# Attention's output projection: from row products over whole blocks to seven block products

## The chip, the cores and the metric

One core of one Trainium2 chip runs the whole program in one launch. TensorE (PE) multiplies, VectorE (DVE) and ScalarE (ACT) work on tiles in SBUF and PSUM, GpSimd (POOL) and SyncE (SP) mostly issue transfers. Each engine runs its own list of instructions, and semaphores join the lists. The metric is device time of one execution in microseconds, the median of several runs.

## The reference, cut to what matters

A decoder trunk of two layers on one sequence of 512 rows and 1024 columns, in fp32. Layer 0 mixes with gated linear attention, layer 1 with strictly causal stick-breaking attention of 16 heads of 64; each is followed by a squared-ReLU MLP (1024 to 4096 to 1024) and LayerNorms. The change is in layer 1:

```python
z = jnp.einsum('bqhd,bkhd->bhqk', q_blk, k_blk) * scale
log_1m = jnp.where(mask, jax.nn.log_sigmoid(-z), 0.0)
rev = lax.cumsum(log_1m, axis=3, reverse=True)
log_w = jax.nn.log_sigmoid(z) + (rev - log_1m)
w = jnp.where(mask, jnp.exp(log_w), 0.0)
outs.append(jnp.einsum('bhqk,bkhd->bqhd', w, v_blk))
...
mix = o.reshape(B, S, D).astype(h.dtype) @ sb_w_o[j]
h = layer_norm(DEEPNORM_ALPHA * h + mix, ln_g[layer, 0], ln_b[layer, 0])
```

The product that is changed is the last but one line: o (512 x 1024) times sb_w_o (1024 x 1024). Its result is added to the residual rows h, which are then normed, transposed and multiplied by the MLP's first weights.

## The kernel before, in words

Every large product is made of three matmuls for each pair of 128-deep operands: a number is split into a high part (ACT's copy to a shorter format, `hi`) and a low part (DVE's subtraction, `lo`), and high times high, high times low and low times high are summed in a PSUM bank. `put` does this for a result in PSUM, `split_tile` for a weight tile of 128 x 1024. There are eight PSUM banks, handed out in turn by `bank()`. `unit()` gives a tile of 4 x 512 columns (they show as T in the profile), `chain()` one of 512 (c).

The 16 heads are taken as eight pairs, 0 to 7. For each pair there are: `keys` and `queries` (products by 128 columns of weights), `scores` (PE, six banks), `weights` (DVE masks the diagonal blocks in PSUM, ACT takes two sigmoids, DVE scans them into the attention weights c), `turn` (PE transposes c into a bank, ACT copies it to `wt`) and `outputs` (PE multiplies the values by wt; the result is the transposed attention output of 128 columns for 512 rows). The loop over p issues, in this order: pair p's turn, woven into PE work that does not depend on it; the weights of pair p+1; the outputs of pair p. `outputs` ended in a `put`. For p up to 5 the turn is woven into the queries of pair p+2. For pairs 6 and 7 there are no more queries, and the first half of the output projection fills their turns: for each tile of 128 rows t, `rows(oA, t, ...)` multiplies the four finished pairs 0 to 3 (oA) by a 512 x 512 block of sb_w_o, 12 matmuls of 128x512, 48 in each turn. After pair 7, `part2(t)` does the second half, pairs 4 to 7, with 24 matmuls for each tile t, and `finish` norms that tile's rows (statistics and centring on DVE, a reciprocal root on POOL) while PE goes on with the next; `turn_affine` then transposes the normed rows (L231), applies gain and bias in ACT's copy (L234) and splits them by `put`, for the MLP's first product `up(0)`. The order from `by_tiles` was: tile 0, tile 1, transposes of 0, tile 2, transposes of 1, tile 3, transposes of 2; tile 3's transposes were done within up(0).

The order on each engine follows the code, save that the splits of a weight tile are set further ahead than their line in it, between the copies and scans that stand there.

## Time and profile before

| | |
|---|---|
| median of 3 runs | 1115.32 us (1114.44 to 1115.41) |
| the profiled execution | 1115.04 us |
| its span, first to last instruction | 1113.3 us |
| granted TensorE clock, mean | 0.999 |
| PE busy | 1105.4 us (99%), 5515 matmuls and transposes |
| DVE busy | 805.8 us (72%) |
| ACT busy | 559.4 us (50%) |
| POOL busy | 131.5 us (12%) |

Matmul rows are pipelined: each reads about 0.39 us, and the start of the next comes earlier than its end, so durations of PE are taken from starts. Times below count from the span's start. In the profile of before, matmul lines are L93 to L95 (the three passes), L934 (scores), L968 (transposes of weights), L982 (outputs), L231 (transposes of normed rows); ACT's are L70 (hi of a weight), L98 (hi of `put`), L955 and L956 (sigmoids), L973 (wt) and L234; DVE's are L72 (lo of a weight), L99 (lo of `put`), L951 (masks), L959 (scans), L167 and L169 (adds to h).

### The profile page before, as it was taken

The page shows a single profiled execution, that of the slowest core. Times are in us where ns is not written, and L with a number is a line of the kernel's source. Part 1 is how long each engine was busy: PE and PEld are TensorE (multiplying, and loading weights), DVE is VectorE, ACT ScalarE, POOL GpSimd, SP SyncE. Part 2 cuts the span into 40 slices and gives each one's busy share as a digit, 9 for nine tenths or more (in the row PEclk, how much of TensorE's full clock was granted, in tenths as well). Part 3 has the DMA queues.
Part 4 walks back from the last instruction along what each step waited for, and adds up shares of the span by engine and source line. Part 5 has one row for each costly group of instructions (what it writes and reads, how often), then busy time and mean ns, then how long its engine had stood idle before and what let it go on. Part 6 is the DMA issues. An engine that isn't in the chain of part 4 may idle for free.

```text
span 1113.3 us, 14363 instructions
## 1 busy us (share of the span) xinstructions
PE 1105.4 (99%) x5515; PEld 916.0 (82%) x5515; DVE 805.8 (72%) x1017; ACT 559.4 (50%) x839; POOL 131.5 (12%) x167
## 2 busy tenths in 40 slices
PE   9999999999999999999999999999999999999997
PEld 7888888898888888888888777778988888888885
DVE  4677639957966856858899786767389767667677
ACT  4455437653533534536675566655445435336363
POOL 1011222200000100122302010001200000001222
PEclk9999999999999999999999999999999999999999
DMA  7441399492670770787845422111946806706773
GB/s 239 132 133 57 114 253 215 123 298 96 188 208 19 199 209 26 195 204 132 245 98 158 116 85 95 58 55 51 291 120 202 234 33 176 221 19 190 183 124 89
DMA packets 108632, 163.81 MB, mean 147 GB/s; under 512 B 13018, under 2 KB 37978, under 8 KB 108564
## 3 DMA queue, kind: packets, MB, share of 16 engines
q1 hardware_dynamic: 85684, 118.34, 32.4%
q0 software_dynamic: 20416, 39.85, 20.4%
q10 hardware_dynamic: 2464, 4.72, 1.1%
q8 instruction: 43, 0.70, 0.2%
q14 instruction: 25, 0.20, 0.1%
HBM read 157.64 MB, written 3.15 MB: 144 GB/s over the span
## 4 chain that ended last, share of the span: by engine, by line
PE 91%; DMA 5%; DVE 1%; issue 1%; POOL 1%; SPq 0%; ACT 0%; POOLq 0%; DVEq 0%
PE ps L355 28%; PE ps L93 18%; PE ps L94 18%; PE ps L95 18%; DMA B<-in_gla_w_o_dram 4%; PE ps L796 3%; PE ps L982 2%; PE ps L968 2%; PE ps L934 2%; PE ps L231 1%; DMA h<-in_x_dram 0%; PE ps L584 0%; POOL B L314 0%; PE ps L121 0%; DVE lo L72 0%
## 5 line engine op out<-in xcount | busy, mean ns | idle before, releaser
L355 PE MATMUL ps<-hi,T 128*128 128x512 f32 x1008 | 313.2, 390 | 0.1
L93 PE MATMUL ps<-T,hi 128*128 128x512 f32 (+1 forms) x776 | 290.1, 374 | 0.0
L94 PE MATMUL ps<-T,hi 128*128 128x512 f32 (+1 forms) x776 | 287.1, 370 | 0.1
L95 PE MATMUL ps<-T,lo 128*128 128x512 f32 (+1 forms) x776 | 286.9, 370 | 0.0
L72 DVE TENSOR_TENSOR lo<-raw,hi 128x1024 fp32r<-128x1024 f32 x130 | 158.0, 1221 | 115.0 <-ACT hi L70 114.7
L355 PEld LDWEIGHTS ps<-hi,T 128*128 128x128 f32 x1008 | 188.9, 188 | 40.0 <-DVE T L99 0.6
L70 ACT ACTIVATE hi<-raw 128x1024 fp32r<-128x1024 f32 x130 | 137.6, 1063 | 166.8 <-PE ps L94 59.2
L70 ACT ACTIVATE hi<-B 128x1024 fp32r<-128x1024 f32 x118 | 124.4, 1059 | 171.2 <-PE ps L94 104.2
L72 DVE TENSOR_TENSOR lo<-B,hi 128x1024 fp32r<-128x1024 f32 x118 | 142.9, 1222 | 84.7 <-ACT hi L70 84.5
L355 PE MATMUL ps<-lo,T 128*128 128x512 f32 x504 | 196.1, 389 | 0.0
L95 PEld LDWEIGHTS ps<-T,lo 128*128 128x128 f32 x776 | 146.2, 188 | 24.8
L93 PEld LDWEIGHTS ps<-T,hi 128*128 128x128 f32 x776 | 146.2, 188 | 24.4 <-issue 0.9
L94 PEld LDWEIGHTS ps<-T,hi 128*128 128x128 f32 x776 | 146.4, 189 | 23.7 <-DVE T L99 0.4
L314 POOL DMA_DIRECT2D B<-in_mlp_w_down_dram x52 | 63.0, 1259 | 544.7 <-DMA B<-in_mlp_w_down_dram 343.6
L355 PEld LDWEIGHTS ps<-lo,T 128*128 128x128 f32 x504 | 94.6, 188 | 19.6
L169 DVE TENSOR_TENSOR h<-h,ps 128x512 f32<-128x512 f32 x110 | 74.9, 682 | 6.9 <-PE ps L95 4.0
L93 PE MATMUL ps<-hi,T 128*128 128x512 f32 x192 | 77.4, 403 | 0.0
L95 PE MATMUL ps<-hi,T 128*128 128x512 f32 x192 | 75.3, 392 | 0.0
L94 PE MATMUL ps<-lo,T 128*128 128x512 f32 x192 | 75.1, 391 | 0.0
L99 DVE TENSOR_TENSOR T<-s,T 128x1024 fp32r<-128x1024 f32 (+1 forms) x50 | 53.4, 1069 | 9.3 <-ACT T L98 9.3
L98 ACT ACTIVATE T<-s 128x1024 fp32r<-128x1024 f32 (+1 forms) x50 | 47.0, 946 | 21.2 <-DVE s L721 14.1
L959 DVE TENSOR_TENSOR_SCAN c<-r,c 128x384 f32<-128x384 f32 (+2 forms) x64 | 48.4, 807 | 3.8 <-ACT c L956 3.8
(190 smaller groups left out, 1195.4 us busy)
## 6 DMA issues: line engine op xcount, KB each, us to landing
raw<-in_mlp_w_up_dram SPq DMA_DIRECT2D x64, 512.0 KB, 5.6
B<-in_mlp_w_down_dram SPq DMA_DIRECT2D x64, 512.0 KB, 5.5
B<-in_mlp_w_down_dram POOLq DMA_DIRECT2D x52, 512.0 KB, 8.0
raw<-in_gla_w_in_dram SPq DMA_DIRECT2D x20, 512.0 KB, 3.9
raw<-in_mlp_w_down_dram SPq DMA_DIRECT2D x16, 512.0 KB, 4.6
B<-in_gla_w_o_dram POOLq DMA_DIRECT2D x14, 512.0 KB, 8.2
raw<-in_kv_w_dram SPq DMA_DIRECT2D x12, 512.0 KB, 4.7
B<-in_gla_w_o_dram SPq DMA_DIRECT2D x8, 512.0 KB, 6.1
```

The costliest lines, as they stand in the source:

```text
L70: keep(nc.scalar.activation(hi, raw, AF.Copy))
L72: keep(nc.vector.tensor_tensor(lo, raw, hi.bitcast(F32), op=ALU.subtract))
L93: keep(nc.tensor.matmul(ps, lhsT=a[0], rhs=b[0], start=first, stop=False))
L94: keep(nc.tensor.matmul(ps, lhsT=a[0], rhs=b[1], start=False, stop=False))
L95: keep(nc.tensor.matmul(ps, lhsT=a[1], rhs=b[0], start=False, stop=last))
L98: keep(nc.scalar.activation(hi, ps, AF.Copy))
L99: keep(nc.vector.tensor_tensor(lo, ps, hi.bitcast(F32), op=ALU.subtract))
L169: nc.vector.tensor_tensor(h, h, ps, op=op)
L314: nc.gpsimd.dma_start(out=b.rearrange("p (a b) -> p a b", a=2), in_=weights(k, h, j), accum_op=ALU.add)
L355: nc.tensor.matmul(banks[s], lhsT=a(k, s)[x], rhs=b[k][y], start=opens and (k, x, y) == (0, 0, 0), stop=closes and (k, x, y) == (3, 1, 0), ...
L796: nc.tensor.matmul(banks[s], lhsT=a(k, s)[x], rhs=b[k][w], start=opens and (k, x, w) == (0, 0, 0), stop=closes and (k, x, w) == (3, 1, 0), ...
L959: nc.vector.tensor_tensor_scan(down, r[:, at][:, ::-1], down, 0.0, op0=ALU.mult, op1=ALU.add)
```

## The change

The 512 x 1024 by 1024 x 1024 product is taken as 2 x 2 blocks: a11, a21 are rows 0 to 255 and 256 to 511 of pairs 0 to 3; a12, a22 the same of pairs 4 to 7; sb_w_o is cut into four 512 x 512 blocks. Seven products of sums of blocks, each of 2 row tiles x 4 depths x 3 passes = 24 matmuls, replace eight of 24.

- Product 1 (a11 by the first block) runs in pair 6's turn, and its two banks are added into or taken off all four row tiles, both halves (eight adds). Transposes of the turn are issued at its steps 3, 4, 6 and 7 (`FILL`). Product 7 (a11 - a21 by a sum of blocks) runs in pair 7's turn.
- The other five, 120 matmuls, run in `project()`, in the order second, sixth, fifth, third, fourth. The row tiles are complete after the fifth (tiles 2 and 3, one half), the third (half of tiles 0, 1) and the fourth. The order handed to `finish` is now: rows 0, 1, 2, transposes of 0, rows 3, transposes of 1; the transposes of 2 and 3 are done within up(0).
- The outputs of pairs 0 to 3 are copied by ACT to o1, unsplit. Those of pairs 4 to 7 are split by `put` as before, and copied once more by ACT to o2. Sums of blocks are taken by DVE from o1 and o2 (`minus`, and a subtraction) and split into five operands (`first`, `seventh`, `sixth`, `fifth`, `third`).
- The sums of weight blocks are built by transfers: `fetch` brings a block to a buffer by a plain transfer on SP, and the following blocks are added by accumulating transfers on POOL. One buffer b22 (two tiles of 128 x 1024, d) takes three, one after another, with its splits between; the buffers of the last k and q take one.
- k and q tiles hold high and low part in one; `differences` uses the d tiles, and there are five c buffers instead of nine.

```diff
+        def outputs(self, steps):
 
             ops = bank()
             for s, (j, i, e) in enumerate(steps):
@@ -983,15 +988,61 @@
                                      lhsT=vs[hd // 8][:, j, DH * (hd % 8):DH * (hd % 8) + DH],
                                      rhs=self.wt[a][:, 512 * j + P * (i - j):512 * j + P * (e - j)], start=(s == 0),
                                      stop=(s == len(steps) - 1), skip_group_check=True)
-            put(hi, lo, ops)
+            return ops
 
     NP = SBH // 2
     TAKE = {4: 2, 5: 1, 6: 1, 7: 1}
 
+    FILL = {3: 1, 4: 1, 6: 1, 7: 1}
+
     LAST = [(0, 2, 4), (1, 2, 4), (2, 2, 4), (3, 3, 4), (0, 0, 1), (0, 1, 2), (1, 1, 2)]
+    LO, HI = slice(0, 256), slice(256, 512)
+    STEPS = [(s, k) for s in range(2) for k in range(4)]
+    LATER = [(s, k) for s in range(2) for k in range(3)] + [(0, 3), (1, 3)]
+    w_o = lambda k, h, j: block(sb_w_o[0], 512 * k + 256 * h, 512 * j)
+
+    def fetch(bs, k, j, onto=False):
+        for h, b in enumerate(bs):
+            to = b.rearrange("p (a b) -> p a b", a=2)
+            if onto:
+                nc.gpsimd.dma_start(out=to, in_=w_o(k, h, j), accum_op=ALU.add)
+            else:
+                nc.sync.dma_start(out=to, in_=w_o(k, h, j))
+
+    def pieces(bs):
+        got = []
+        for b in bs:
+            hi, lo = split_tile(b, 2)
+            got += [(hi[:, i, :], lo[:, i, :]) for i in range(2)]
+        return got
+
+    def into(u, a, ks):
+
+        put(u[:, ks, LO], u[:, ks, HI], a[:, ks, :])
+
+    def halves(u):
+        return lambda k, s: (u[:, k, P * s:P * s + P], u[:, k, 256 + P * s:256 + P * s + P])
+
+    def run(steps, a, b, banks, opens=True, closes=True, mid=None):
+
+        for n, (s, k) in enumerate(steps):
+            if mid:
+                mid(n)
+            if opens and k == 0:
+                banks[s] = bank()
+            for x, y in ((0, 0), (0, 1), (1, 0)):
+                nc.tensor.matmul(banks[s], lhsT=a(k, s)[x], rhs=b[k][y], start=opens and (k, x, y) == (0, 0, 0),
+                                 stop=closes and (k, x, y) == (3, 1, 0), skip_group_check=True)
+
+    def add(s, banks, i, j, first=False, last=False):
+        hs[2 * i + s].add(j, banks[s], first, last, ALU.subtract if j else ALU.add)
+
+    tt = nc.vector.tensor_tensor
+    minus = lambda out, a, b: nc.vector.scalar_tensor_tensor(out, a, -1.0, b, op0=ALU.mult, op1=ALU.subtract)
+
     pairs = [Pair(p) for p in range(NP)]
-    oA = Split(1)
-    parts = [(oA.hi[0][:, i, :], oA.lo[0][:, i, :]) for i in range(4)]
+    o1 = unit(F32)
+    a11, a21 = o1[:, :, LO], o1[:, :, HI]
     vec, vcols = lnvec(0, 1), lncols(1, 0)
     pairs[0].keys(held[0])
     pairs[0].queries(ps=held[1])
@@ -1007,37 +1058,97 @@
             made = pairs[p].turn()
             pairs[p + 2].queries(lambda k: [next(made, None) for _ in range(TAKE.get(k, 0))])
         else:
-            n = p - (NP - 2)
-            pcs = pieces_512(sb_w_o[0], 0, 4, 512 * n)
             made = pairs[p].turn()
-            for t in range(NT):
-                hs[t].add(n, rows(oA, t, pcs, range(4)), True)
-                for _ in range(((0, 1, 2, 2), (1, 1, 2, 1))[n][t]):
-                    next(made, None)
+            fill = lambda n: [next(made, None) for _ in range(FILL.get(n, 0))]
+            ps = [None, None]
+            if p == NP - 2:
+                run(STEPS, halves(first), pieces_512(sb_w_o[0], 0, 4, 0), ps, mid=fill)
+                for s in range(2):
+                    for i in range(2):
+                        for j in range(2):
+                            add(s, ps, i, j, True)
+            else:
+                run(STEPS, halves(seventh), b7, ps, mid=fill)
+                for s in range(2):
+                    for j in range(2):
+                        add(s, ps, 1, j)
+            for _ in made:
+                pass
         if p + 1 < NP:
             pairs[p + 1].weights()
         if p == 1:
             differences(1)
         if p in (1, 2):
             hs[1 + p].affine(vec, tc.keep_in_program_order)
-        if p in (4, 6):
-            u = unit(F32R)
-            parts += [(u[:, i, :], u[:, 2 + i, :]) for i in range(2)]
-        pairs[p].outputs(*parts[p], LAST if p == NP - 1 else [(j, j, NT) for j in range(NT)])
-    pcs = [pieces_512(sb_w_o[0], 512, 4, 512 * n) for n in range(2)]
+        ops = pairs[p].outputs(LAST if p == NP - 1 else [(j, j, NT) for j in range(NT)])
+        if p < 4:
+            nc.scalar.activation(o1[:, p, :], ops, AF.Copy)
+        else:
+            if p == 4:
+                o2, o2h, o2l = unit(F32), unit(F32R), unit(F32R)
+                a12, a22 = o2[:, :, LO], o2[:, :, HI]
+            put(o2h[:, p - 4, :], o2l[:, p - 4, :], ops)
+            nc.scalar.activation(o2[:, p - 4, :], ops, AF.Copy)
+        if p == 3:
+            first = unit(F32R)
+            into(first, a11, slice(0, 4))
+            b22 = wide()
+            fetch(b22, 1, 1)
+            fetch(b22, 0, 1, True)
+        if p == NP - 3:
+            seventh = unit(F32R)
+            for h in range(2):
+                ks, less = slice(2 * h, 2 * h + 2), chain().rearrange("p (a b) -> p a b", a=2)
+                tt(less, a11[:, ks, :], a21[:, ks, :], op=ALU.subtract)
+                put(seventh[:, ks, LO], seventh[:, ks, HI], less)
+            b5 = [both(tag).bitcast(F32).rearrange("p a b -> p (a b)") for tag in ("k", "q")]
+            fetch(b5, 0, 0)
+            fetch(b5, 0, 1, True)
+        if p == NP - 2:
+            b7 = pieces(b22)
+            fetch(b22, 0, 0, True)
+            sixth, fifth = unit(F32R), unit(F32R)
+        if p >= NP - 2:
+            ks = slice(0, 3) if p == NP - 2 else slice(3, 4)
+            tt(a22[:, ks, :], a22[:, ks, :], a21[:, ks, :], op=ALU.subtract)
+            minus(a11[:, ks, :], a22[:, ks, :], a11[:, ks, :])
+            into(sixth, a11, ks)
+            into(fifth, a22, ks)
     h3T = Split()
+    whole = lambda c0: lambda k, s: tuple(o[:, k, c0 + P * s:c0 + P * s + P] for o in (o2h, o2l))
+
+    def project():
+
+        xs, zs, ws = ([None, None] for _ in range(3))
+        run(LATER, whole(0), pieces_512(sb_w_o[0], 512, 4, 0), xs)
+        for s in range(2):
+            add(s, xs, 0, 0, last=True)
+        b6 = pieces(b22)
+        fetch(b22, 1, 0, True)
+        minus(a12, a12, a11)
+        run(STEPS, halves(sixth), b6, zs, closes=False)
+        for s in range(2):
+            add(s, zs, 1, 0)
+        run(STEPS, halves(fifth), pieces(b5), zs, False, False)
+        for s in range(2):
+            add(s, zs, 1, 1, last=True)
+        third = unit(F32R)
+        into(third, a12, slice(0, 4))
+        b3 = pieces_512(sb_w_o[0], 512, 4, 512)
+        b4 = pieces(b22)
+        for s in range(2):
+            run(STEPS[4 * s:4 * s + 4], halves(third), b3, zs, False)
+            add(s, zs, 0, 1, last=True)
+            yield s
+        for s in range(2):
+            run(STEPS[4 * s:4 * s + 4], whole(256), b4, ws)
+            add(s, ws, 1, 0, last=True)
+            yield 2 + s
+            yield ~s
 
     vec = lnvec(1, 0)
 
-    def part2(t):
-        c = slice(P * t, P * t + P)
-        pss = [bank(), bank()]
-        for n, k in ((0, 0), (0, 1), (0, 2), (1, 0), (0, 3), (1, 1), (1, 2), (1, 3)):
-            mm3(pss[n], tuple(o[:, c] for o in parts[4 + k]), pcs[n][k], k == 0, k == 3)
-        for n in range(2):
-            hs[t].add(n, pss[n], False, True)
-
-    late = finish(by_tiles(part2), vcols, hs, h3T, chain)
+    late = finish(project(), vcols, hs, h3T, chain)
     sbx.__exit__(None, None, None)
 
     def done1(steps, work, *_):
```

Three places show what moves. The first is DVE between pair 6's scans (L959 before, L964 now) and the masks of pair 7's scores (L951, L956). Before (T_6117 is the low part of pair 5's outputs, the h rows are the adds of the four row tiles):

```order
L99 TENSOR_TENSOR T_6117<-ps_6300,T_6117 128x512
L167 SCALAR_TENSOR_TENSOR h_1637<-h_1637,ps_6323 128x512
L167 SCALAR_TENSOR_TENSOR h_1638<-h_1638,ps_6337 128x512
L167 SCALAR_TENSOR_TENSOR h_1639<-h_1639,ps_6359 128x512
L72 TENSOR_TENSOR lo_6628<-raw_6624,hi_6626 128x1024
L167 SCALAR_TENSOR_TENSOR h_1640<-h_1640,ps_6386 128x512
L72 TENSOR_TENSOR lo_6634<-raw_6630,hi_6632 128x1024
L951 TENSOR_TENSOR ps_6414<-ps_6414,low 128x128
L951 TENSOR_TENSOR ps_6415<-ps_6415,low 128x128
```

Now, where T_6114 is that low part, c_6300 and c_6304 are the two halves of a11 - a21, T_6299 is the seventh operand and d_5928 is b22:

```order
L99 TENSOR_TENSOR T_6114<-ps_6287,T_6113 128x512
L1102 TENSOR_TENSOR c_6300<-T_5008 128x512
L167 SCALAR_TENSOR_TENSOR h_1637<-h_1637,ps_6326 128x512
L1102 TENSOR_TENSOR c_6304<-T_5008 128x512
L99 TENSOR_TENSOR T_6299<-c_6300,T_6299 128x2x256
L167 SCALAR_TENSOR_TENSOR h_1637<-h_1637,ps_6326 128x512
L99 TENSOR_TENSOR T_6299<-c_6304,T_6299 128x2x256
L167 SCALAR_TENSOR_TENSOR h_1639<-h_1639,ps_6326 128x512 x2
L167 SCALAR_TENSOR_TENSOR h_1638<-h_1638,ps_6353 128x512 x2
L167 SCALAR_TENSOR_TENSOR h_1640<-h_1640,ps_6353 128x512 x2
L956 TENSOR_TENSOR ps_6395<-ps_6395,low 128x128
L956 TENSOR_TENSOR ps_6396<-ps_6396,low 128x128
```

Between T and the masks stood four adds and two weight splits; now twelve operations of 512 columns stand there, and the two weight splits come behind the masks, one ahead of the first scan and one ahead of the last.

The second place is ACT in pair 7's turn, from the copy of pair 6's outputs to the last wt copies. Before:

```order
L98 ACTIVATE T_6480<-ps_6481 128x512 [waits PE_49]
L973 ACTIVATE wt_6518<-ps_6520 128x4x128 [waits PE_49]
L973 ACTIVATE wt_6519<-ps_6540 128x4x128 [waits PE_49]
L973 ACTIVATE wt_6518<-ps_6560 128x3x128 [waits PE_49]
L973 ACTIVATE wt_6518<-ps_6560 128x128
L973 ACTIVATE wt_6519<-ps_6567 128x3x128 [waits PE_49]
L973 ACTIVATE wt_6519<-ps_6567 128x128
L70 ACTIVATE hi_6874<-raw_6872 128x1024 [waits DMAHW2_49,PE_49]
```

Now (T_6112 is o2, hi_6671 the high part of the weight sum in the k tile, T_6483 and T_6484 the sixth and the fifth operand; L978 are the wt copies):

```order
L978 ACTIVATE wt_6502<-ps_6512 128x4x128 [waits PE_49]
L1091 ACTIVATE T_6112<-ps_6461 128x512 [waits DVE_49]
L70 ACTIVATE hi_6671<-k_6308 128x1024 [waits DMASW6_49,PE_49]
L978 ACTIVATE wt_6501<-ps_6525 128x3x128 [waits PE_49]
L978 ACTIVATE wt_6501<-ps_6525 128x128
L978 ACTIVATE wt_6502<-ps_6535 128x3x128 [waits PE_49]
L98 ACTIVATE T_6483<-T_5008 128x3x256 [waits DVE_49]
L98 ACTIVATE T_6484<-T_6112 128x3x256 [waits Activation_49]
L978 ACTIVATE wt_6502<-ps_6535 128x128
L978 ACTIVATE wt_6501<-ps_6549 128x2x128 [waits PE_49]
L978 ACTIVATE wt_6502<-ps_6549 128x2x128
```

A copy to o2 that waits for DVE, a weight split and two high parts came among the wt copies; the two splits of weights of before, of which the first row is shown, follow the wt copies. In pair 6's turn the o2 copy and the two halves of T_6299 stand among the wt copies in the same way.

The third place is PE at the end of the projection. Before, the last part2 matmuls, the transposes of tile 2 and up(0)'s first:

```order
L93 MATMUL ps_6807<-hi_6632,T_6480 128x512
L94 MATMUL ps_6807<-lo_6634,T_6480 128x512
L95 MATMUL ps_6807<-hi_6632,T_6480 128x512
L231 MATMUL ps_6845<-ident,h_1639 128x128 x4
L231 MATMUL ps_6857<-ident,h_1639 128x128 x4
L93 MATMUL ps_6896<-T_6636,hi_6874 128x256
L94 MATMUL ps_6896<-T_6637,hi_6874 128x256
L95 MATMUL ps_6896<-T_6636,lo_6876 128x256
```

Now the fourth product's last matmuls, the transposes of tile 1 (h_1638) and up(0) with the first transposes of tile 2 (h_1639):

```order
L1034 MATMUL ps_6820<-hi_6728,T_6113 128x512
L1034 MATMUL ps_6820<-lo_6730,T_6113 128x512
L1034 MATMUL ps_6820<-hi_6728,T_6114 128x512
L231 MATMUL ps_6843<-ident,h_1638 128x128 x4
L231 MATMUL ps_6855<-ident,h_1638 128x128 x4
L93 MATMUL ps_6894<-T_6580,hi_6872 128x256
L93 MATMUL ps_6895<-T_6580,hi_6872 128x256
L93 MATMUL ps_6896<-T_6580,hi_6872 128x256
L93 MATMUL ps_6897<-T_6580,hi_6872 128x256
L231 MATMUL ps_6947<-ident,h_1639 128x128 x3
L94 MATMUL ps_6894<-T_6581,hi_6872 128x256
L95 MATMUL ps_6894<-T_6580,lo_6874 128x256
```

Tile 1's transposes, which had a row tile's 24 matmuls behind them, now stand directly ahead of up(0), and those of tile 2 are in up(0).

More of the change, by code (lines that the diff above doesn't have):

```diff
@@ L887, in chain, with wide @@
     def chain():
-        return sbp.tile([P, S], F32, tag="c", bufs=9, name=nm("c"))
+        return sbp.tile([P, S], F32, tag="c", bufs=5, name=nm("c"))
+    def wide():
+        return [sbp.tile([P, 2 * S], F32, tag="d", bufs=2, name=nm("d")) for _ in range(2)]
     def differences(n):
-        v, shifted = vs[n], [chain() for _ in range(NT)]
+        v, shifted = vs[n], [d[:, at] for d in wide() for at in (slice(0, S), slice(S, 2 * S))]
         nc.gpsimd.memset(shifted[0][0:1, :], 0.0)
@@ L903, in yoco_kernel, with both @@
     HALVES = ((A0, A1), (A1, A0))
+    def both(tag):
+        return sbp.tile([P, 2, S], F32R, tag=tag, bufs=2, name=nm(tag))
     class Pair:
@@ L909, in __init__ @@
             self.p = p
-        def part(self, tag):
-            return sbp.tile([P, S], F32R, tag=tag, bufs=2, name=nm(tag))
         def keys(self, ps=None):
             ps = ps or cols(h2T, piece_128(kv_w, P * self.p))
-            self.k = self.part("kh"), self.part("kl")
+            k = both("k")
+            self.k = k[:, 0, :], k[:, 1, :]
             put(*self.k, ps)
@@ L920, in queries @@
             ps = ps or cols(h2T, piece_128(sb_w_q[0], P * self.p), mid)
-            self.q = qh, ql = self.part("qh"), self.part("ql")
+            q = both("q")
+            self.q = qh, ql = q[:, 0, :], q[:, 1, :]
             nc.scalar.activation(qh, ps, AF.Copy, scale=DH ** -0.5)
@@ L974, in turn @@
                 yield
-        def outputs(self, hi, lo, steps):
+        def outputs(self, steps):
             ops = bank()
```

## Prediction

> **What bounds the kernel now.** I read the page's totals first, then the stretches around the change, then each engine's order of time in them.
>
> ```profile
> PE 1105.4 (99%) x5515; PEld 916.0 (82%) x5515; DVE 805.8 (72%) x1017; ACT 559.4 (50%) x839; POOL 131.5 (12%) x167
> PE 91%; DMA 5%; DVE 1%; issue 1%; POOL 1%; SPq 0%; ACT 0%; POOLq 0%; DVEq 0%
> ...
> 712.40:730.20 17.80, 17.80 (x109) 13.98 (x108) 12.60 (x21) 10.69 (x22) 0.00 (x0) 1.00 0.09 31
> 730.20:748.10 17.90, 17.90 (x111) 13.96 (x110) 12.32 (x22) 10.96 (x26) 0.00 (x0) 1.00 0.19 60
> 748.10:775.00 26.90, 26.90 (x150) 22.28 (x149) 18.72 (x29) 12.47 (x27) 2.38 (x6) 1.00 0.13 40
> ```
>
> PE is 91% of the chain that ended last. The three stretches are pair 6's part, pair 7's part and the rest of the projection (length, then busy time of PE, PEld, DVE, ACT, POOL, granted clock): PE never stops in them, while DVE works 12.6 of 17.8 us and ACT 10.7. So a matmul removed is time gained, and a wait that PE meets is time lost one for one: later stages have no idle PE time to absorb it. The DMA share of 0.09 to 0.19 leaves transfers out of the bound.
>
> The PE rows give the price of a matmul and the points that PE reaches:
>
> ```profile
> 719.01 0.39 PE L93 MATMUL ps<-hi,T 128*128 128x512 f32 x1
> 721.73 0.39 PE L93 MATMUL ps<-hi,T 128*128 128x512 f32 x1
> 730.22 0.50 PE L934 MATMUL ps<-kh,qh 64*128 64x512 f32 x2
> 732.33 2.37 PE L982 MATMUL ps<-wt,T 128*64 128x512 f32 x16
> 747.56 0.60 PE L968 MATMUL ps<-ident,c 128*128 128x128 f32 x4
> 748.08 2.39 PE L982 MATMUL ps<-wt,T 128*64 128x256 f32 x28
> 750.40 0.50 PE L93 MATMUL ps<-hi,T 128*128 128x512 f32 x1
> 774.14 1.03 PE L231 MATMUL ps<-ident,h 128*128 128x128 f32 x8
> 774.93 0.36 PE L93 MATMUL ps<-T,hi 128*128 128x256 f32 x1
> ```
>
> Twelve matmuls lie between the first two starts: 2.72 / 12 = 0.227 us each, though a row reads 0.39. The rest are pair 7's scores, pair 6's outputs, pair 7's last transposes, its outputs, the start of the rest of the projection, the last transposes ahead of up(0), and up(0)'s first matmul.
>
> **The gain.** Seven products of 24 replace 192 matmuls by 168: 24 x 0.227 = -5.5 us. But each of the last two turns goes from 48 to 24, so PE asks for the next thing 24 x 0.227 = 5.5 us earlier in pair 6's turn and 10.9 us earlier at the end of pair 7's, and gives 5.5 us back afterwards. Without any wait PE would reach pair 7's scores at 724.8, its last transposes at 736.7, its outputs at 737.2, the remaining products at 739.5. What must be ready there is made by DVE and ACT:
>
> ```profile
> 719.34 3.59 DVE L959 TENSOR_TENSOR_SCAN c<-r,c 128x384 f32<-128x384 f32 x6
> 722.85 0.67 DVE L99 TENSOR_TENSOR T<-ps,T 128x512 fp32r<-128x512 f32 x1
> 723.43 1.27 DVE L167 SCALAR_TENSOR_TENSOR h<-h,ps 128x512 f32<-128x512 f32 x2
> ...
> 730.92 1.22 DVE L72 TENSOR_TENSOR lo<-raw,hi 128x1024 fp32r<-128x1024 f32 x1
> 732.06 0.49 DVE L951 TENSOR_TENSOR ps<-ps,low 128x128 f32<-128x128 f32 x2
> 733.56 1.23 DVE L959 TENSOR_TENSOR_SCAN c<-r,c 128x512 f32<-128x512 f32 x1 [1.01 <-ACT c L956]
> ...
> 738.03 2.42 DVE L959 TENSOR_TENSOR_SCAN c<-r,c 128x384 f32<-128x384 f32 x4
> 740.38 0.66 DVE L99 TENSOR_TENSOR T<-ps,T 128x512 fp32r<-128x512 f32 x1
> ```
>
> In before, pair 7's masks (732.06) begin 1.8 us after its scores and its last scan ends at 740.4, 7 us before PE transposes it at 747.56. That slack is what the change spends.
>
> **The waits.** I walk the new order with these durations.
>
> *DVE ahead of pair 7's masks.* From the low part T at 722.85 to the masks there now stand thirteen 128x512 operations (T, two a-differences and their low parts, eight h adds), each 0.60 (722.85 to 723.43, and 1.27 for two): 13 x 0.60 = 7.8, so masks at 730.7, 5.9 us after PE wants to write those scores. From masks to the last scan's end before took 740.4 - 732.1 = 8.3, of which 1.0 was waiting on ACT; two weight splits (1.2 each, 1.14 apart) now lie between the scans: 8.3 - 1.0 + 2.3 = 9.6, less some overlap with ACT. The last scan ends at about 740.2, the same instant as before, while PE's need for it has moved to 736.7 plus the waits so far.
>
> ```profile
> 720.48 0.73 ACT L98 ACTIVATE T<-ps 128x512 fp32r<-128x512 f32 x1
> 723.05 0.60 ACT L973 ACTIVATE wt<-ps 128x512 f32<-128x512 f32 x1 [1.85 <-PE ps L968]
> ...
> 728.09 1.06 ACT L70 ACTIVATE hi<-raw 128x1024 fp32r<-128x1024 f32 x1 [0.66 <-PE ps L95]
> 729.45 1.06 ACT L70 ACTIVATE hi<-raw 128x1024 fp32r<-128x1024 f32 x1 [0.30 <-PE ps L95]
> 730.42 1.19 ACT L973 ACTIVATE wt<-ps 128x384 f32<-128x384 f32 x4
> ```
>
> *ACT in pair 6's turn.* The new copy of the outputs to o2 waits for DVE's T (done 723.5), and what stands behind it waits too: copy 0.5, half of the seventh operand's high part 0.5, a wt copy 0.5, the other half (its a-difference, DVE's fourth operation, ends at 725.3) to 725.9, a weight split 0.96, then the wt copies that free the next score bank, at 727.5. PE stands in pair 7's scores at 725.4: **2.1 us**. Two more wt copies (0.55), a split (0.96) and the last wt pair (0.5) end at 729.5; PE is ready for outputs at 728.8: **0.8 us**.
>
> *Pair 7's turn.* PE then comes to the last transposes at 736.7 + 2.9 = 739.4 or so; the scan ends 740.2: **0.9 us**. At pair 7's outputs (740.5) ACT has just got past its next o2 copy, which waited for DVE's T behind the last scan (740.8): copy 0.5, split 0.96, three wt columns 0.4 give 742.9: **2.4 us**, and **0.2** for the next. Inside these outputs the high parts of the sixth and fifth operands stand ahead of three wt copies. They wait for two h adds and two 768-wide DVE subtractions after T (2 x 0.6 + 2 x 0.9 past 740.8: 743.9), take 0.7 each, and the copies come at 745.7: **1.1 us** in three pieces. Outputs end at about 746.5 rather than 739.5.
>
> *The five products after.* They run without a wait. An accumulating transfer and its neighbours land in:
>
> ```profile
> B<-in_gla_w_o_dram POOLq DMA_DIRECT2D x14, 512.0 KB, 8.2
> raw<-in_sb_w_o_dram SPq DMA_DIRECT2D x8, 512.0 KB, 3.5
> ```
>
> The second sum in the shared buffer is issued as soon as pair 7's product weights have been split out of it, ahead of pair 6's scores at 712, and is read at 725.9; the third is issued after DVE's two splits (732.3 and 739.7) and read at 756.4 and 757.8, 8 us beyond the 8.2 it takes; the sum in the k and q tiles is issued near 719 and read at 741. They cost nothing on this path. On POOL's queue the last of them stands at 740, ahead of the LayerNorm work of the first tile near 768; on SP's the two plain fetches of the k/q sum stand between weights of up(0) that are read near 762 and later. Early in the attention the shifted copies of the second half wait sooner, which may hold one w_q fetch: 0 to 0.7 us at pair 3's keys; I take 0.
>
> *LayerNorm into up(0).* Before, 24 matmuls stood between the transposes of tile 1 and of tile 2, and only tile 3 went into up(0). Now tile 1's transposes stand directly ahead of up(0), whose first matmul reads them:
>
> ```profile
> 775.09 1.89 ACT L234 ACTIVATE c<-ps,bcol,gcol 128x128 f32<-128x128 f32 x5
> 776.80 0.69 ACT L98 ACTIVATE T<-c 128x512 fp32r<-128x512 f32 x1
> 778.45 1.08 POOL L183 TENSOR_SCALAR ve<-mv 128x1 f32<-128x1 f32 x1 [7.82 <-DVE mv L182]
> 779.62 0.57 POOL L184 TENSOR_TENSOR rs<-ve,mhalf 128x1 f32<-128x1 f32 x1
> 780.22 0.81 DVE L190 TENSOR_SCALAR h<-h,mv,rs 128x1024 f32<-128x1024 f32 x1 [0.77 <-POOL rs L184]
> ```
>
> From the first affine row to the end of T took 2.4 us (775.09 to 777.49); the second half of the transposes (0.3) runs beside it: **2.1 us**. DVE then still owes the low part, behind an h add 0.6, a weight split 1.14, statistics 0.6, another low part 0.6, and itself 0.7 (from about 777.5): 781.3, and PE, after four matmuls and three transposes, waits **2.0 us** for it. Ahead of both, tile 1's own centring stands behind two weight splits (2.3) and three other operations on DVE: **0.9 us**. Before, the 24 matmuls (5.5 us) hid all of this.
>
> Sum: waits 2.1 + 0.8 + 0.9 + 2.4 + 0.2 + 1.1 + 0.9 + 2.1 + 2.0 = 12.5; with -5.5 it is +7.0. The profiled execution took 1115.04 (its span 1113.3 and what lies around it), 0.28 under the median of the runs shown: 1115.04 + 7.0 = **1122.0 us**. Each wait is a difference of two walked times, good to some 0.3, and they partly share causes: the likeliest case alone runs from 1118.5 (waits of 9) to 1124.5 (waits of 14.3 and the 0.7).
>
> **Rivals.** *Faster: the waits are hidden.* ACT and DVE are idle 40% and 30% of these stretches, and 24 fewer matmuls are real: 1115.04 - 5.5 = 1109.6. It needs the last scan done by 736.7 and wt copies not behind DVE; the order of rows speaks against both. Deciding point: under 5.5 us of waits in all. 0.12.
>
> *No change: only DVE's chain binds.* If ACT's copies pass quickly (PE does not need the score bank or wt that early), PE waits once, 740.2 - 736.7 = 3.5, and for the late low part in up(0), 2.0: -5.5 + 5.5, so 1115.0. For it: DVE's times are the firmest. Against: ACT is served in order. 0.09.
>
> *Worse: the clock drops, or a sum lands late.* The trace lets the clock fall only after PE has stopped for good:
>
> ```profile
> 1106.00:1108.00 2.00, 1.42 (x4) 0.35 (x2) 1.23 (x2) 0.95 (x2) 1.75 (x2) 1.00 0.62 121
> 1108.00:1110.00 2.00, 0.00 (x0) 0.00 (x0) 1.41 (x3) 0.24 (x1) 0.00 (x0) 1.00 0.78 301
> 1110.00:1114.00 4.00, 0.00 (x0) 0.00 (x0) 0.00 (x0) 0.00 (x0) 0.00 (x0) 0.71 0.31 114
> ```
>
> PE ended at 1107.4, and the clock was still 1.00 up to 1110, 2.6 us later, then 0.71 on average. My longest wait is 2.4, but between 739.4 and 746.5 PE would stand for 4.6 of 7.1 us. If that counts as a stop, ten us of products at 0.71 cost 10 x (1/0.71 - 1) = 4.1: 1126. A sum 5 us later than 8.2 costs nothing yet; 10 us later, about 2: 1124. Together 0.05.
>
> The Trainium skill (TensorE: Matmul & The Clock Gate, "What's actually happening") has the clock halve after an idle window of about 3.4 us and recover after as long a busy one; by it a fall here would cost an estimated 1.7 us, 1123.7, and single waits of 2.4 us would leave it alone. The trace agrees that 2.6 us of rest did not lower it; no run here yet shows a fall between matmuls.
>
> **How the numbers follow.** The likeliest case (0.74) gives 1122.0. Faster 0.12, no change 0.09, worse 0.05. About 0.2% (2.2 us) is what a measurement can tell from no change here; the likeliest case's low end (1118.5) is beyond it, so slower is 0.74 + 0.05 and a little of the middle, 0.78; same 0.10; faster 0.12. The range leaves out the faster case and half of the worse one: 1114.5 to 1125.
>
> **What would show it.** In the profile after: PE idle about 12 us more in its waits, at the scores and outputs lines behind ACT's wt copies, at the last transposes behind the scan, and at the first up(0) matmuls behind ACT's and DVE's T; thirteen DVE operations of 0.60 between the scan and the masks; attention outputs 7 ending about 1.6 us before 748.08 rather than 10. Wrong would be: PE busy again 17.8 of 17.8 in these stretches (then 1109.6), or POOL's transfers named as the releaser of a PE wait or of ACT's split.

## The result, and the profile after

The changed kernel takes 1125.42 us (median of 4 runs, 1124.23 to 1126.34) against 1115.28 for the kernel before (1114.44 to 1115.41): ratio 1.0092, 95% interval 1.0074 to 1.0109, so 10.1 us slower. The forecast was 7 us, with a range up to 1125.0. The profiled execution took 1126.34, its span 1124.5; the mean granted clock fell from 0.999 to 0.995.

From the page of the changed kernel, the engines' totals and the shares of the chain that ended last:

```profile
PE 1106.3 (98%) x5491; PEld 915.0 (81%) x5491; DVE 823.4 (73%) x1040; ACT 571.8 (51%) x857; POOL 141.2 (13%) x175
PE 88%; DVE 7%; ACT 1%; issue 1%; DMA 1%; POOL 1%; SPq 0%; POOLq 0%; DVEq 0%; ACTq 0%
```

PE has 24 matmuls less, yet is busy 0.9 us longer. DVE's share of the chain rose from 1% to 7%, by near 70 us of the span. Some 20 of them lie between 589 and 616 us, where the chain runs back from the wait at 629.83 that is shown below. Lines moved by five or less: scores are now L939, transposes of weights L973, wt L978, outputs L987, masks L956, scans L964.

What PE's weight loads wait for, grouped (us in all, times, longest; rows that name no instruction as the releaser are left out):

```profile
PEld ps L987 <- ACT wt L978: 3.4, 4, 1.4
PEld ps L93 <- ACT T L98: 2.9, 2, 2.5
...
PEld ps L94 <- DVE T L99: 2.1, 2, 1.7
PEld ps L939 <- ACT wt L978: 2.0, 1, 2.0
PEld ps L93 <- DVE q L928: 1.8, 1, 1.8
```

Four of the five are places that the prediction named: outputs and scores behind ACT's wt, up(0) behind ACT's and DVE's T. The last row, a q, was not in its sum. The weight loads idle a little longer than the matmuls themselves. PE's own rows at these places (start, length, in brackets the idle time before and its releaser):

```profile
629.83 0.50 PE L93 MATMUL ps<-T,hi 128*128 128x512 f32 x1 [1.51 <-DVE q L928]
...
729.52 1.48 PE L939 MATMUL ps<-k,q 64*128 64x384 f32 x17 [1.59 <-ACT wt L978]
731.56 4.07 PE L987 MATMUL ps<-wt,T 128*64 128x512 f32 x16 [0.56 <-ACT wt L978]
...
744.76 2.27 PE L987 MATMUL ps<-wt,T 128*64 128x256 f32 x18 [1.18 <-ACT wt L978]
747.63 1.20 PE L987 MATMUL ps<-wt,T 128*64 128x128 f32 x10 [0.60 <-ACT wt L978]
...
777.86 1.09 PE L231 MATMUL ps<-ident,h 128*128 128x128 f32 x8 [0.71 <-DVE h L190]
781.20 0.74 PE L93 MATMUL ps<-T,hi 128*128 128x256 f32 x4 [2.25 <-ACT T L98]
783.71 0.58 PE L94 MATMUL ps<-T,hi 128*128 128x256 f32 x1 [1.44 <-DVE T L99]
...
786.22 0.41 PE L93 MATMUL ps<-T,hi 128*128 128x256 f32 x1
...
789.42 0.42 PE L93 MATMUL ps<-T,hi 128*128 128x256 f32 x1
790.28 0.28 PE L93 MATMUL ps<-T,hi 128*128 128x256 f32 x1
...
791.35 0.28 PE L93 MATMUL ps<-T,hi 128*128 128x256 f32 x1
```

Two things show here besides waits. Pair 6's outputs, 16 matmuls, take 4.07 us; before they took 2.37. And up(0)'s first matmuls run 0.213 us apart (786.22 to 789.42, 15 steps), then 0.119 apart (790.28 to 791.35, 9 steps). Windows of the same run (length; busy PE, PEld, DVE, ACT, POOL; granted clock, DMA share, GB/s), cut at the times at which the clock changes, give the reason:

```profile
728.30:731.72 3.42, 1.64 (x19) 1.44 (x21) 3.42 (x7) 3.21 (x8) 0.00 (x0) 1.00 1.10 196
731.72:735.13 3.41, 3.41 (x12) 1.23 (x12) 3.41 (x6) 2.06 (x4) 0.60 (x1) 0.50 0.08 13
...
779.50:782.92 3.42, 1.06 (x7) 0.82 (x7) 3.42 (x6) 3.42 (x9) 0.00 (x0) 1.00 0.01 4
782.92:786.33 3.41, 2.62 (x12) 2.62 (x13) 2.64 (x6) 0.74 (x2) 1.11 (x2) 0.50 0.44 150
786.33:789.74 3.41, 3.41 (x18) 3.41 (x18) 0.64 (x2) 0.00 (x0) 0.00 (x0) 0.50 0.64 205
731.00:748.00 17.00, 14.66 (x82) 9.68 (x82) 16.96 (x27) 11.96 (x27) 2.39 (x2) 0.90 0.43 73
```

The granted clock halves twice: from 731.72 to 735.13, and from 782.92 to 789.74, which is 3.41 us and twice 3.41. Beside the first fall DVE is busy 16.96 of 17.00 us. The chain of waits of the same run, cut to the attention's end, says the same: from 716.6 on it lies almost wholly on DVE.

```profile
718.70 1.23 DVE c L964
...
729.03 3.68 DVE h L167 x6
...
745.84 1.58 ACT T L98 x2
```

The difference of the two profiled executions, taken stretch by stretch from the starts of PE's rows in each:

| stretch | forecast | measured | what is in it |
|---|---|---|---|
| start of the program | 0 | +0.4 | first transfer |
| attention up to pair 6's scores | 0 | +1.6 | wait 1.51 for q at 629.83 |
| pair 6's turn | -5.5 | -5.4 | 24 matmuls less |
| pair 7's scores | +2.9 | +2.7 | waits 1.59, 0.56 |
| pair 6's outputs | 0 | +1.7 | half clock |
| pair 7's turn | -2.2 | -4.2 | 24 less; wait 1.18 |
| pair 7's outputs | +1.3 | +1.7 | wait 0.60, small ones |
| projection up to up(0) | +7.7 | +7.9 | 24 more; waits 0.71, 2.25 |
| up(0) on | +2.8 | +5.4 | transposes 0.8, wait 1.44, half clock |
| sum | +7.0 | +11.7 | |

The sum goes to the start of PE's last matmuls; what follows them is about half a microsecond shorter in the change. The profiled run of after is its slowest and that of before below its median: 11.3 between these two, 10.1 between the medians.

### The profile page after: what moved, and what is told of

It reads as the page before. It is cut to its first block, busy times and chain, and to the rows that moved or that the text cites. A ratio compares the mean times of both kernels' runs of the same rounds, so it can differ in the third digit from the quotient of the medians.

```text
span 1124.5 us, 14374 instructions
## 1 busy us (share of the span) xinstructions
PE 1106.3 (98%) x5491; PEld 915.0 (81%) x5491; DVE 823.4 (73%) x1040; ACT 571.8 (51%) x857; POOL 141.2 (13%) x175
## 4 chain that ended last, share of the span: by engine, by line
PE 88%; DVE 7%; ACT 1%; issue 1%; DMA 1%; POOL 1%; SPq 0%; POOLq 0%; DVEq 0%; ACTq 0%
PE ps L355 29%; PE ps L93 17%; PE ps L94 17%; PE ps L95 17%; PE ps L796 2%; DVE c L964 1%; PE ps L1034 1%; DVE lo L72 1%; PE ps L973 1%; PE ps L987 1%; PE ps L939 1%; PE ps L231 1%; DVE h L169 1%; DVE h L167 1%; DVE T L99 0%
## 5 line engine op out<-in xcount | busy, mean ns | idle before, releaser
L355 PE MATMUL ps<-hi,T 128*128 128x512 f32 x1008 | 313.6, 390 | 0.1
L72 DVE TENSOR_TENSOR lo<-raw,hi 128x1024 fp32r<-128x1024 f32 x128 | 155.7, 1221 | 103.3 <-ACT hi L70 99.0
L355 PE MATMUL ps<-lo,T 128*128 128x512 f32 x504 | 196.2, 389 | 0.0
L169 DVE TENSOR_TENSOR h<-h,ps 128x512 f32<-128x512 f32 x116 | 78.7, 682 | 3.0 <-PE ps L355 2.4
L93 PE MATMUL ps<-hi,T 128*128 128x512 f32 x128 | 51.4, 402 | 0.0
L719 ACT ACTIVATE s<-ps 128x512 f32<-128x512 f32 x64 | 38.0, 594 | 25.9 <-PE ps L95 25.2
L964 DVE TENSOR_TENSOR_SCAN c<-r,c 128x384 f32<-128x384 f32 (+2 forms) x64 | 48.5, 807 | 2.5 <-ACT c L961 2.5
L95 PE MATMUL ps<-hi,T 128*128 128x512 f32 x128 | 50.3, 393 | 0.0
```

The lines of the kernel that those rows point to most:

```text
L72: keep(nc.vector.tensor_tensor(lo, raw, hi.bitcast(F32), op=ALU.subtract))
L93: keep(nc.tensor.matmul(ps, lhsT=a[0], rhs=b[0], start=first, stop=False))
L95: keep(nc.tensor.matmul(ps, lhsT=a[1], rhs=b[0], start=False, stop=last))
L169: nc.vector.tensor_tensor(h, h, ps, op=op)
L355: nc.tensor.matmul(banks[s], lhsT=a(k, s)[x], rhs=b[k][y], start=opens and (k, x, y) == (0, 0, 0), stop=closes and (k, x, y) == (3, 1, 0), ...
L719: nc.scalar.activation(s2[:, f, :], pss[f], AF.Relu)
```

## The experiments

Ratios are to the kernel before, on the same chip.

**Is the second clock fall worth 2.5 us?** 13 matmuls into an unused bank, behind the last transposes, fill part of the wait ahead of up(0).

```diff
...
             yield ~s
+        warm(13, whole(256)(3, 1)[0], b4[3][0])
```

> The changed kernel with 13 matmuls of 128x512 added between tile 1's transposes and up(0), into a bank that nobody reads. They need nothing that is late, and take 13 x 0.227 = 3.0 us of the 2.25 + 1.44 us that PE idles there. Theory A (the idle time lowers the granted clock): the rows of up(0), 0.212 us apart from 783.7 to 789.6, are 0.119 apart again, the granted clock of that stretch is 1.00 instead of 0.50, and the kernel is about 2.7 us faster: 1122.7. Rival B (up(0) is slow for another reason: transfers running at full share, or the weight loads): the rows stay at 0.212 and the time at 1125.4, or up to 0.5 above it.

Measured: 1122.94 us (1121.34 to 1124.18), ratio 1.0071 (1.0054 to 1.0088), 2.5 less than the change itself, as expected with the clock as the cause. Its first late wait of up(0), and a window behind it:

```profile
781.31 0.39 PE L94 MATMUL ps<-T,hi 128*128 128x256 f32 x1 [0.95 <-DVE T L99]
...
783.00:785.00 2.00, 2.00 (x19) 2.00 (x18) 1.57 (x2) 0.00 (x0) 0.00 (x0) 1.00 0.00 0
```

From the end of the wait for the centring (777.86 in the change, 775.47 here) to the arrival of the low T it is 5.85 us there and 5.84 here: the data come no earlier. The clock stays at 1.00, and from that point to the last transposes (1117.13 and 1112.11) it is 333.4 us there and 330.8 here. These 2.6 us are the clock's and not the wait's. (This execution met neither the early wait at 629.83 nor one for the first transfer, which is why its times are 2.4 us ahead.)

**Is the early wait due to the second half's subtractions?** `differences(1)` one pair later.

```diff
-        if p == 1:
+        if p == 2:
             differences(1)
```

> The changed kernel with the value differences of the second eight heads taken after pair 2 instead of after pair 1. Theory A: the 1.51 us wait of PE at pair 3's keys or queries (629.83, for DVE's low part of q) came from these differences, which hold a weight split and with it a fetch: it goes, 1123.9, nothing else moves. Rival B: the differences only move the wait to pair 3's or 4's part, or the shared buffer's first fetch, which waits for them, comes late: 1125.4 or more.

Measured: 1124.29 us (1123.62 to 1125.2), ratio 1.0080 (1.0065 to 1.0095), 1.1 less; single executions of the two kernels overlap (1124.23 to 1126.34 for the change). PE goes from the outputs straight into the keys:

```profile
625.74 2.37 PE L987 MATMUL ps<-wt,T 128*64 128x512 f32 x16
628.05 0.50 PE L93 MATMUL ps<-T,hi 128*128 128x512 f32 x1
```

In the changed kernel the way to that wait reads, on DVE, on SP's queue and on ACT:

```profile
616.74 1.89 DVE L904 TENSOR_TENSOR T<-T,d 128x512 f32<-128x512 f32 x3
...
620.95 1.22 DVE L72 TENSOR_TENSOR lo<-raw,hi 128x1024 fp32r<-128x1024 f32 x1
...
622.24 0.37 SPq L64 DMA_DIRECT2D raw<-in_sb_w_q_dram  x1
...
626.86 1.06 ACT L70 ACTIVATE hi<-raw 128x1024 fp32r<-128x1024 f32 x1 [2.97 <-DMA raw<-in_sb_w_q_dram]
```

The subtractions, and four operations of a row tile behind them, stand on DVE ahead of a weight split (620.95; in before 616.74). The split frees the buffer for the w_q fetch, which is issued at 622.24 instead of 617.99 and lands too late. In this run it is issued at 616.46.

**Do the fifth and sixth operands cost their place in pair 7's outputs?** All of both is made after pair 7 rather than three quarters before it.

```diff
-        if p >= NP - 2:
-            ks = slice(0, 3) if p == NP - 2 else slice(3, 4)
+        if p == NP - 1:
+            ks = slice(0, 4)
```

> The changed kernel with the sixth and fifth operands made in one piece after pair 7's outputs, not in two (three quarters in pair 7's turn). Theory A: their high parts, which wait for DVE, hold the last wt copies: pair 7's outputs, 4.0 us from first start to the next product, take 2.4 to 2.8, of which 0.5 to 1.0 comes back as a wait of the sixth product: 1124.4 to 1125.0. Rival B: the copy to o2 and the weight split ahead of the wt copies set that end: outputs stay at 4.0 us, and the later operands add 1 us: 1126.4.

Measured: 1123.54 us (1121.95 to 1124.22), ratio 1.0070 (1.0055 to 1.0085).

```profile
743.39 2.93 PE L987 MATMUL ps<-wt,T 128*64 128x256 f32 x28 [1.95 <-ACT wt L978]
...
779.54 1.22 PE L93 MATMUL ps<-T,hi 128*128 128x256 f32 x4 [2.55 <-ACT T L98]
```

Wait and outputs together take 4.88 us instead of 5.25 (743.58 to 748.83 in the rows of the change): the pieces within the outputs became one wait ahead of them. So the operands' place is worth 0.4 of the 1.9 us by which this median is lower. The rest lies elsewhere: up(0) waited for ACT's T only, its clock fall lasted 3.41 us instead of 6.83, and the early wait, which this edit does not touch, was 0.46 in this execution.

**Does the seventh operand block pair 7's scores?** It is made at the end of pair 4 instead of pair 5.

```diff
-        if p == NP - 3:
+        if p == 4:
             seventh = unit(F32R)
...
```

> The changed kernel with the seventh operand (a11 - a21 and its split) made after pair 4 instead of after pair 5, so that four of the thirteen DVE operations and two ACT operations leave pair 6's turn. Theory A (these hold the wt copies and the scans, and the clock then falls): the waits in pair 7's scores and before pair 6's outputs fall from 2.15 us to about 1.5, pair 6's outputs (4.0 us at clock 0.50 to 0.68) go back to 2.3 if the clock no longer falls, and 0.5 to 1 us comes back at pair 7's outputs: about 1123.5. Rival B (the eight adds to h alone bind there): waits stay at 2, the clock falls as before: 1125.2.

Measured: 1126.07 us (1125.51 to 1126.91), ratio 1.0096 (1.0081 to 1.0111): nothing gained.

```profile
728.00 1.49 PE L939 MATMUL ps<-k,q 64*128 64x384 f32 x17 [0.35 <-DVE h L167]
730.27 2.37 PE L987 MATMUL ps<-wt,T 128*64 128x512 f32 x16 [0.79 <-ACT wt L978]
...
742.88 0.65 PE L987 MATMUL ps<-wt,T 128*64 128x256 f32 x2 [2.28 <-ACT wt L978]
745.68 3.94 PE L987 MATMUL ps<-wt,T 128*64 128x256 f32 x26 [1.49 <-ACT wt L978]
...
737.00:748.00 11.00, 7.23 (x39) 4.83 (x39) 10.93 (x17) 8.37 (x19) 0.00 (x0) 0.88 0.21 38
```

The wait at the scores fell from 1.59 to 0.35, pair 6's outputs ran in 2.37 at full clock, and all of it came back at pair 7's outputs: waits of 2.28 and 1.49 and a clock fall there. Neither theory had this. DVE is busy 10.93 of 11.00 us. A wait that goes at one place while the same DVE work stands ahead of the next is only moved.

**How long must PE stop for the clock to fall?** In the kernel before, one matmul is made to wait behind a row of ACT copies at the start of the second half's products: three copies, then six.

```diff
+        if t == 0:
+            a, b, x = bank(), bank(), chain().bitcast(F32R)
+            nc.tensor.matmul(a, lhsT=parts[4][0][:, c], rhs=pcs[0][0][0], start=True, stop=True)
+            for _ in range(3):
+                nc.scalar.activation(x, a, AF.Copy)
+            nc.tensor.matmul(b, lhsT=x[:, 0:P], rhs=pcs[0][0][0], start=True, stop=True)
```

> The kernel before, with PE stopped once in a quiet place: after tile 0's 24 matmuls of the second half of the projection, one extra matmul, three ACT copies of 512 columns of its bank, one behind the other (0.48 us each), and a matmul that reads the last. PE should idle about 1.9 us there. Theory A (the clock falls when PE has idled for most of some 3.4 us): the clock stays at 1.00 and the time is the stop plus the two matmuls, 1115.3 + 2.4 = 1117.7. Rival B (any stop of over 1.5 us lowers it, as the 1.59 us in pair 7's scores seemed to): clock at 0.50 for some 3 us behind it, 1.5 us more: 1119.2.

Measured: 1118.25 us (seven executions, 1117.70 to 1120.64), ratio 1.0030 (1.0019 to 1.0041), +3.0 us.

```profile
758.58 0.50 PE L1044 MATMUL ps<-hi,c 128*128 128x512 f32 x1 [1.94 <-ACT c L1043]
...
754.41:757.82 3.41, 2.23 (x10) 1.50 (x8) 2.71 (x4) 1.11 (x2) 0.00 (x0) 1.00 0.03 11
757.82:761.23 3.41, 2.65 (x11) 2.17 (x12) 1.07 (x3) 0.68 (x2) 0.80 (x2) 1.00 0.02 5
```

> The same with six ACT copies: PE idles about 3.4 us. Theory A: the clock falls to 0.50 for 3 to 6 us behind the stop, matmuls of 512 columns are 0.45 us apart there, and the kernel is 3.9 us of stop and matmuls plus 1.7 to 3 slower: 1121 to 1122. Rival B (only many small waits, not one stop, do it; or the fall in the changed kernel came from something else): clock 1.00, 1119.2.

Measured: 1121.17 us (two executions, 1120.64 and 1121.71), ratio 1.0054 (1.0034 to 1.0074).

```profile
759.66 0.77 PE L1044 MATMUL ps<-hi,c 128*128 128x512 f32 x1 [3.83 <-ACT c L1043]
...
756.31:759.72 3.41, 0.06 (x1) 0.06 (x1) 1.73 (x4) 3.14 (x6) 0.80 (x2) 1.00 0.00 0
759.72:763.13 3.41, 3.41 (x8) 2.76 (x9) 0.00 (x0) 0.00 (x0) 0.00 (x0) 0.50 0.02 5
```

In the two profiled executions a single stop of 1.94 us left the clock at 1.00, and one of 3.83 halved it for 3.41 us. The windows are cut where the clock can change (the last section shows how that is known). The stop of 1.94 lies across such a cut, 1.18 us before it and 0.76 behind, so PE is busy 2.23 and 2.65 us in the two windows; the stop of 3.83 empties one. What 1.94 us inside a single window do was not tried. The difference of the two medians, 2.9 us, is 1.9 of longer stop, which leaves about 1 for the clock.

**Can POOL take subtractions off DVE?** `tt`, the plain subtractions of the operands, goes to POOL.

```diff
-    tt = nc.vector.tensor_tensor
+    tt = nc.gpsimd.tensor_tensor
```

> The changed kernel with the plain subtractions of blocks (two of 512 columns, one of 768, one of 256) on POOL instead of DVE: 2.4 us of DVE work leave the stretch from pair 6's scans to the projection, in which DVE worked 16.96 of 17.00 us. Theory A (DVE's work there is the bound, and what is taken from it comes off the waits): 1.5 to 2.5 us less, 1123.4. Rival B (ACT's order or the adds to h bind, or POOL is slow at it): the waits of PE only move from pair 7's scores to its outputs, 1125 to 1126.

Measured: 1131.25 us (1129.69 to 1133.05), ratio 1.0140 (1.0123 to 1.0157), 5.8 more than the change: a miss.

```profile
722.63 1.76 POOL L1102 TENSOR_TENSOR c<-T 128x512 f32<-128x512 f32 x1
724.64 2.21 POOL L1102 TENSOR_TENSOR c<-T 128x512 f32<-128x512 f32 x1
...
749.66 1.11 PE L987 MATMUL ps<-wt,T 128*64 128x256 f32 x2 [4.99 <-ACT wt L978]
```

POOL takes 1.76 and 2.21 us, beside transfers that it issues at the same time, for what takes DVE 0.60. ACT's high parts, with wt copies behind them, wait for POOL's results, and the clock falls three times, for 6.83 us each.

**How much of the loss do the moves win back together?** They are: the two of the second and fourth run, operands and their subtractions as in the third and on POOL, the o2 copy ahead of `put`, and the transposes of tiles 0 and 1 set into the fourth product.

```diff
...
-            put(o2h[:, p - 4, :], o2l[:, p - 4, :], ops)
             nc.scalar.activation(o2[:, p - 4, :], ops, AF.Copy)
+            put(o2h[:, p - 4, :], o2l[:, p - 4, :], ops)
...
+        run(STEPS[:4], whole(256), b4, ws)
+        yield ~0
+        add(0, ws, 1, 0, last=True)
+        yield 2
+        run(STEPS[4:6], whole(256), b4, ws)
+        yield ~1
+        run(STEPS[6:], whole(256), b4, ws)
```

> The changed kernel with all the moves at once: differences of the values after pair 2, the seventh operand after pair 4, plain subtractions on POOL, the copy to o2 ahead of the split of the outputs, sixth and fifth operands in one piece after pair 7's outputs, and the transposes of tiles 0 and 1 set 12 and 6 matmuls before the end of the projection. Theory A (what DVE and ACT do in these turns, in order, is the whole loss, and the clock falls with it): waits worked out as 1.0 in pair 7's scores, 1.0 in its turn, 1.6 at its outputs, 0.8 at tile 0, 2.0 and 1.5 in up(0), 7.9 in all, less the 5.5 of the matmuls: 1117.7, and 2 more if the clock still falls once. Rival B (the same work has to be done before the same point, so waits only move): 1121 or more.

Measured: 1119.80 us (1118.69 to 1120.33), ratio 1.0041 (1.0026 to 1.0056).

```profile
739.96 2.94 PE L987 MATMUL ps<-wt,T 128*64 128x256 f32 x28 [1.12 <-ACT wt L978]
...
776.42 0.79 PE L93 MATMUL ps<-T,hi 128*128 128x256 f32 x4 [2.17 <-ACT T L98]
```

5.6 of the 10.1 us go, with 1.12 left at pair 7's outputs and 2.17 at up(0), and one clock fall of 3.41 us (from 776.99). It is still 4.5 slower than before. The subtractions changed their engine as well as their place, and which of the moves did what was not taken apart.

**Is it DVE's work that binds the turns?** The eighth kernel with two of product 1's eight adds; the other six adds are left out, so it doesn't compute the whole product.

```diff
-                    for i in range(2):
-                        for j in range(2):
-                            add(s, ps, i, j, True)
+                    add(s, ps, 0, 0, True)
```

> The kernel with all the moves (e8, 1119.8), leaving out six of the eight additions of product 1 to h (its result is added into one half of two row tiles only): 6 x 0.60 = 3.6 us of DVE work less ahead of pair 7's masks. Theory A (with ACT's order mended, DVE is what PE waits for in the two turns): the wait in pair 7's scores, the small ones in its turn and part of that at its outputs go, 2 us in all: 1117.8. Rival B (ACT's wt copies or transfers set those waits): within 0.5 us of e8, 1119.3 to 1120.3.

Measured: 1116.73 us, ratio 1.0013 (1.0004 to 1.0023), 3.1 less than the eighth.

```profile
738.25 2.94 PE L987 MATMUL ps<-wt,T 128*64 128x256 f32 x28 [0.38 <-ACT wt L978]
```

Six operations of 0.60, 3.6 us of DVE's time, are worth 3.1 us between the medians. In the two profiled executions the way from pair 6's scores to up(0) is 1.9 us shorter (61.96 against 63.84), as theory A had it; the rest lies between executions. So DVE's adds are paid for in these turns. They also hold product 1's banks: the eighth's wait of 0.35 in pair 7's scores names an add to h, and it is gone here. DVE's time and the banks were not told apart.

**Cover for up(0).** The eighth kernel with 10 spare matmuls ahead of up(0), as in the first experiment.

```diff
...
         yield 3
+        warm(10, whole(256)(3, 1)[0], b4[3][0])
```

> The kernel with all the moves (e8, 1119.8) and ten matmuls of 128x512 (2.3 us), read by nobody, ahead of up(0), where PE idles 2.17 us. Theory A (e8's only fall of the clock, 0.60 to 0.83 between 775 and 781, comes from that wait): the clock stays at 1.00, about 1.5 us less, 1118.3. Rival B (no more than the wait itself is lost there): 1119.8 or up to 0.3 above.

Measured: 1118.16 us, ratio 1.0029 (1.0019 to 1.0040), the fastest of the whole kernels with seven products, 1.6 less than the eighth; in the two profiles, from up(0)'s first matmul on, it is 1.0 (332.50 against 333.47). Behind the wait the clock is 1.00, where the eighth has 0.60 in the same window:

```profile
778.00:781.00 3.00, 3.00 (x28) 3.00 (x27) 2.75 (x4) 1.38 (x2) 0.21 (x1) 1.00 0.00 0
```

Then real work in that place: the row halves change roles and the products are cut up, so that 36 matmuls stand behind tile 1.

```diff
-    a11, a21 = o1[:, :, LO], o1[:, :, HI]
+    a11, a21 = o1[:, :, HI], o1[:, :, LO]
...
+        run(STEPS[:4], halves(third), b3, zs, False)
+        add(0, zs, 0, 1, last=True)
+        yield 2
+        yield ~1
+        run(STEPS[4:], halves(third), b3, zs, False)
...
```

> The kernel with all the moves, and the projection in another order: the two row halves change roles, so that tiles 0 and 1 are complete after half of the second, the sixth, the fifth and the fourth product, and 36 matmuls (half of the second, the third) stand behind tile 1's last add instead of 24. Theory A (the LayerNorm waits into up(0) are a matter of the matmuls that stand behind tile 1): the waits of 2.17 and 0.35 in up(0) and of 0.86 at tile 0 go, and the fall of the clock with them, about 4.5 us; the sixth operand is now wanted 12 matmuls after pair 7's outputs instead of 24, 2.5 to 3 us of new waits: 1118 to 1118.5. Rival B (DVE is behind by its own work, wherever the matmuls stand): the waits only come elsewhere, 1120 or more.

Measured: 1124.10 us, ratio 1.0080 (1.0065 to 1.0095): a miss, since operands and rows are now needed earlier than they are made.

```profile
749.24 0.50 PE L1034 MATMUL ps<-hi,T 128*128 128x512 f32 x1 [2.59 <-ACT T L98]
...
782.28 1.33 PE L231 MATMUL ps<-ident,h 128*128 128x128 f32 x5 [1.97 <-DVE h L190]
```

## Why the prediction had the waits right, the clock wrong, and was short by 3.4 us

*Right: the gain.* Pair 6's turn became 5.4 us shorter, forecast 5.5 (24 x 0.227).

*Right: who waits for whom.* PE meets ACT's wt copies at pair 7's scores (1.59 + 0.56 against 2.1 + 0.8, the stretch +2.7 against +2.9) and DVE's and ACT's T and centring ahead of and in up(0) (0.71, 2.25, 1.44 against 0.9, 2.1, 2.0). ACT's wt copies stand behind DVE's work, as argued; the ninth experiment, in the eighth's order, shows that DVE's adds are paid for. The rival in which DVE and ACT hide it all, and the one in which only two waits appear, are out. No wait of PE names an accumulating transfer.

*Wrong: the clock left out of the likeliest case.* The rival of a dropping clock, given 0.05 together with late sums, came true twice. The step that failed took the end of the program, where 2.6 us without PE left the clock at 1.00, as the measure for waits of at most 2.4, and looked for a fall between 739.4 and 746.5 alone. It fell at 731.72 and 782.92, behind waits of 1.59 and 0.56 and of 2.25 and the start of 1.44. The end of the program could not be that measure:

```profile
1104.81:1108.23 3.42, 2.61 (x6) 0.68 (x4) 2.55 (x4) 1.88 (x4) 2.02 (x3) 1.00 0.74 150
1108.23:1111.64 3.41, 0.00 (x0) 0.00 (x0) 1.18 (x3) 0.01 (x1) 0.00 (x0) 1.00 0.79 295
```

In before, PE ended at 1107.4 in a window in which it had been busy 2.61 us, and the clock fell at 1111.64, when the next window was over. So 1.00 at 1110 did not mean that a stop of 2.6 us is harmless; it meant that the window had not ended.

The second fall cost 2.6 us, as the first experiment shows. The first cost 1.7 on pair 6's outputs, and most of it came back in pair 7's turn: there DVE set the pace (16.96 of 17.00 us), so the slower PE found the scan already done (0.9 forecast, none met) and waited 1.18 where 2.4 were forecast. The fourth experiment fits: it had no fall at pair 6's outputs, and as much was lost at pair 7's. No run took that fall away alone.

The Trainium skill (TensorE: Matmul & The Clock Gate, "What's actually happening") has the clock halve after a window of about 3.4 us of idle PE. The traces agree on the length, 3.41 us, and on the half, 0.50. They do not agree that PE must be idle throughout: it was busy 1.64 and 1.06 us in the windows ahead of the two falls, whose longest single waits are 1.59 and 2.25 us. The estimate taken from it, 1.7 us for one fall, fits the first; the second lasted two windows, 6.83 us.

*Wrong: "0 to 0.7 us at pair 3's keys; I take 0".* The place and the w_q fetch were right; the wait was 1.51 in the profiled execution, 0.46 in the third run's and none in the first's, with the same order there. From the fetch's issue to ACT's split of it were 4.62, 3.50 and 3.33 us in these three, so the wait hangs on how fast the fetch lands. With the fetch earlier the median falls by 1.1 us (second experiment).

Forecast 1122.0; with the two terms, 2.5 of median in the first experiment and 1.1 in the second, it would have been 1125.6, against 1125.42 measured. That this fits so closely is partly luck: the first fall's 1.7 us and the 2.0 us that pair 7's turn gave back are in neither term and nearly cancel. The 0.4 at the start of the program is a wait for the first rows of x that differs between executions, and the split of pair 7's waits between ACT and DVE was not taken apart further.

One sign of the prediction was misread by itself: it set the end of pair 7's outputs, 746.5, against their start before, 748.08. They ended at 750.40 before and at 748.83 in the change.

*What stays of the loss.* The moves together win back 5.6 of the 10.1 us (eighth experiment), spare matmuls 1.6 more (tenth), and 2.9 are left. In this order the seven products' adds and subtractions fill a DVE that the last pairs' scans need; no kernel tried was faster than the one before.
